# Causal attention on one NeuronCore: the diagonal blocks of a hybrid decoder layer without padding

## The chip, the cores and the metric

The kernel runs on one core of a Trainium2 chip. The metric is the device time of one execution in microseconds (us). Lower is better.

## The reference, cut to what matters

One decoder layer on 2048 tokens of 1024 features, in float32. Sixteen heads of 64 features: eight of forgetting attention (a softmax with a decay added to the logits) and eight of stick-breaking attention (sigmoids and a running product). Both are causal and take the queries in blocks of 128. Around them lie a projection, an output projection, and a gated MLP with a short convolution.

```python
def forgetting_attention(q, k, v, log_f):
    F = jnp.cumsum(log_f, axis=-1)
    ...
        s = jnp.einsum('bhqd,bhkd->bhqk', q_blk, k) * scale
        s = s + F_blk[..., None] - F[:, :, None, :]
        s = jnp.where(kpos[None, :] <= qpos[:, None], s, -jnp.inf)
        return jnp.einsum('bhqk,bhkd->bhqd', jax.nn.softmax(s, axis=-1), v)

def stick_breaking_attention(q, k, v):
    ...
        strict = kpos[None, :] < qpos[:, None]
        log_one_minus_beta = jnp.where(strict, jax.nn.log_sigmoid(-z), 0.0)
        rest = lax.cumsum(log_one_minus_beta, axis=3, reverse=True) - log_one_minus_beta
        a = jnp.where(strict, jnp.exp(jax.nn.log_sigmoid(z) + rest), 0.0)
        return jnp.einsum('bhqk,bhkd->bhqd', a, v)
```

For a query block t, key blocks beyond t are masked whole: they add nothing to the output.

## The kernel before, in words

The first 1520 us hold the projections and the attention, interleaved on TensorE; then come the output projection and the MLP, which the change does not touch.

**Number types.** Values are float32. Operands of most matmuls are kept in a rounded four-byte type (`fp32r`) as two parts, a rounded one and the rest, so that a product is made of two or three matmuls of that type. Transposes and a few small matmuls (the head variances at L716, the warm-up at L477) use plain float32. The trace names both types f32 on TensorE.

**Units and loops.** `attend` (L697) takes one unit: a kind, a pair of heads and 512 queries. It walks two pairs of query blocks (`j2`, with `j = 2 * tb + j2` from 0 to 7) and both heads of the pair. In all there are 8 pairs of heads, 4 values of `tb`, 2 of `j2` and 2 heads: 128 walks, 64 of them with an even j. One walk handles two query blocks (`qi` 0 and 1, key blocks up to 2j and up to 2j + 1) and accumulates into one PSUM bank `o`.

**Logits** (`logits`, L594): a chunk of up to 512 keys against 128 queries is two matmuls (L596, L597), the two parts of Q against K. The chunk needs `need` columns; in the last chunk `need` is (2j + qi + 1) * 128 less the keys of the chunks before. It is 128 for `qi` 0 where j is even. The matmuls are made `max(need, 2 * P)` wide (L627, L666), so at least 256 columns; the columns beyond `need` are not read. In the stick-breaking heads two sigmoids on ACT (L630, L631), a select on POOL (L633) and a scan on DVE (L636) follow; in the forgetting heads a fused add and minimum on DVE (L675) and an exponential on ACT (L679).

**Value matmuls** (`weighted`, L600): one step takes two key blocks (`kk` 0 and 1) and both query blocks. Four transposes on TensorE (L606) put the weights into a PSUM bank of four slots of 128 columns, in the order (kk 1, q 0), (kk 0, q 0), (kk 0, q 1), (kk 1, q 1). ACT copies them rounded into `at[:, 0]` (L610), DVE writes what is left into `at[:, 1]` (L611). Then four matmuls (L615), two key blocks times two parts, each with V as stationary operand and 256 columns of `at` streamed; for `kk` 1 the columns are the first and the last slot. `at` has three buffers, the PSUM tile `pt` three banks.

**The diagonal.** In the last step of a walk's keys (`kts[0] == 2 * j`) the block (kk 1, q 0) lies above the diagonal and is masked whole. Its transpose is left out, the eviction covers the other 384 columns, and ACT copies 128 zeros per part into its slot from a constant tile `edge` (L609), so that the matmuls of `kk` 1 keep their 256 columns.

**What orders the work.** Program order in `weighted` is as above. Projections of later units are fed in between by `interleave` and `pace` at set shares, some of them behind a logit matmul (`issue_after`, L1061). The order in which each engine finally takes its instructions is planned at build time by the tile framework from a modelled timeline (`schedule_with_timeline_sim=True`, L1758); engines then run in that order and wait on semaphores.

Of the kernel before, what the change touches and what calls it, by code (L numbers as in the profile page):

```python
# [12 lines left out]
AF = mybir.ActivationFunctionType  # L13
# [4 lines left out]
P = 128  # L18
# [16 lines left out]
def kernel(ctx: ExitStack, tc: tile.TileContext, x, c, w_ada, b_ada, g_attn, w_in, b_fgate,  # L35
                      g_out_fox, g_out_sb, w_out, g_mlp, w_up, conv_w, conv_b, w_down, g_final, out):
    nc = tc.nc
# [3 lines left out]
    def f(t):  # L41
        return t.bitcast(F32)
# [29 lines left out]
    edge = const.tile([P, TB + 1], F32, name="edge")  # L72
# [130 lines left out]
    last = {}  # L203
# [13 lines left out]
    b = pv()  # L217
# [6 lines left out]
    for r, src in ((R_GA, g_attn), (R_GM, g_mlp), (R_GF, g_out_fox), (R_GS, g_out_sb), (R_BA, b_ada)):  # L224
        n = src.shape[1] // P
# [368 lines left out]
    def logits(cw, qcols, hl, Q, K):  # L594
        b = qk()
        nc.tensor.matmul(b[:, :cw], Q[:, hl, 0, qcols], K[:, hl, :cw], start=True, stop=False)  # L596
        marks.append(nc.tensor.matmul(b[:, :cw], Q[:, hl, 1, qcols], K[:, hl, :cw], start=False, stop=True).ins)  # L597
        return b

    def weighted(o, kts, blk, V, hl, first, last, diag):  # L600
        b = pt()
        at = sb.tile([P, 2, 2 * 2 * P], F32R, name="at", tag="at", bufs=3)
        order = [(1, 0), (0, 0), (0, 1), (1, 1)]
        for i, (kk, qi) in enumerate(order):
            if not (diag and i == 0):
                nc.tensor.transpose(b[:, i * P:(i + 1) * P], blk(kts[kk], qi), ident)  # L606
        lo = P if diag else 0
        if diag:
            nc.scalar.activation(at[:, :, 0:P], edge[:, 0:2 * P].rearrange("p (a n) -> p a n", n=P), AF.Copy)  # L609
        copies = [nc.scalar.activation(at[:, 0, lo:], b[:, lo:], AF.Copy).ins,  # L610
                  nc.vector.tensor_sub(at[:, 1, lo:], b[:, lo:], f(at[:, 0, lo:])).ins]  # L611
        for kk, kt in enumerate(kts):
            for w in range(2):
                rhs = at[:, w].rearrange("p (s q) -> p s q", q=P)[:, 0:4:3, :] if kk else at[:, w, P:3 * P]
                m = nc.tensor.matmul(o[:, 0:2 * P], V[kt // 4][:, kt % 4, hl, :], rhs,  # L615
                                     start=first and kk == 0 and w == 0, stop=last and kk == 1 and w == 1)
        sums.append(m.ins)
        step[:] = [m.ins] + copies

    def sb_head(j, qc, hl, Q, K, V, o):  # L620
        n = (2 * j + 2 + 3) // 4
        right = [None, None]
        for ch in range(n - 1, -1, -1):
            at = []
            for qi in range(2):
                need = min(512, (2 * j + qi + 1) * P - ch * 512)
                b = logits(max(need, 2 * P), slice((qc + qi) * P, (qc + qi + 1) * P), hl, Q, K[ch])  # L627
                r = sx.tile([P, 512], F32, name="r", bufs=7)
                a = sx.tile([P, 512], F32, name="a", bufs=7)
                nc.scalar.activation(r[:, :need], b[:, :need], AF.Sigmoid)  # L630
                nc.scalar.activation(a[:, :need], b[:, :need], AF.Sigmoid, scale=-1.0)  # L631
                if right[qi] is None:
                    nc.gpsimd.affine_select(out=a[:, need - P:need], in_=a[:, need - P:need], pattern=[[-1, P]],  # L633
                                            base=-1, channel_multiplier=1, compare_op=ALU.is_ge, fill=0.0)
                rev = a[:, 0:need][:, ::-1]
                nc.vector.tensor_tensor_scan(rev, r[:, 0:need][:, ::-1], rev,  # L636
                                             0.0 if right[qi] is None else right[qi][:, 0:1], ALU.mult, ALU.add)
                right[qi] = a
                at.append(a)
            yield  # L640
            nk = min(4, 2 * j + 2 - 4 * ch)
            for m in range(0, nk, 2):
                kts = [4 * ch + m, 4 * ch + m + 1]
                weighted(o, kts, lambda kt, qi: at[qi][:, (kt - 4 * ch) * P:(kt - 4 * ch + 1) * P], V, hl,
                         ch == n - 1 and m == 0, ch == 0 and m == nk - 2, kts[0] == 2 * j)
                yield
# [10 lines left out]
    def fox_head(j, qc, hl, Q, K, V, o, Fb, ls):  # L657
        n = (2 * j + 2 + 3) // 4
        rows_ = []
        for qi in range(2):  # L660
            W = (2 * j + qi + 1) * P
            a = sx.tile([P, S], F32, name="p", bufs=4)
            mn = None
            for ch in range(n):
                need = min(512, W - ch * 512)
                b = logits(max(need, 2 * P), slice((qc + qi) * P, (qc + qi + 1) * P), hl, Q, K[ch])  # L666
                sl = slice(ch * 512, ch * 512 + need)
                m2 = sx.tile([P, 1], F32, name="mn", bufs=8)
                add = Fb[ch]
                if ch == n - 1:  # L670
                    add = px.tile([P, TB], F32, name="Fd", tag="hf_a", bufs=2)
                    mask[:] = [nc.gpsimd.affine_select(
                        out=add[:, :need], in_=Fb[ch][:, :need], pattern=[[-1, need]], base=need - P,
                        channel_multiplier=1, compare_op=ALU.is_ge, fill=BIG).ins]
                nc.vector.tensor_tensor_reduce(out=a[:, sl], in0=b[:, :need], in1=add[:, :need], scale=1.0,  # L675
                                               scalar=3e38 if mn is None else mn, op0=ALU.add, op1=ALU.min,
                                               accum_out=m2)
                mn = m2
            nc.scalar.activation(a[:, 0:W], a[:, 0:W], AF.Exp, scale=-1.0, bias=mn, accum_out=ls[:, hl, qc + qi:qc + qi + 1])  # L679
            rows_.append(a)  # L680
            yield
        for m in range(0, 2 * j + 2, 2):
            weighted(o, [m, m + 1], lambda kt, qi: rows_[qi][:, kt * P:(kt + 1) * P], V, hl, m == 0, m == 2 * j,
                     m == 2 * j)
            yield
# [11 lines left out]
    def attend(kind, p, tb, res, Fbs):  # L697
# [30 lines left out]
        for j2 in range(2):  # L728
            j = 2 * tb + j2
            for hl in range(2):  # L730
                o = pv()
                if kind == "sb":
                    yield from sb_head(j, 2 * j2, hl, Q, K, V, o)
                else:
                    yield from fox_head(j, 2 * j2, hl, Q, K, V, o, Fbs[hl], ls)
                o2 = sb.tile([HD, 2 * P], F32, name="o2", bufs=2)
                step[1] = nc.scalar.activation(o2, o[HD:P, 0:2 * P], AF.Copy).ins
                nc.vector.tensor_add(oT[hl * HD:(hl + 1) * HD, j2 * 2 * P:(j2 + 1) * 2 * P], o[0:HD, 0:2 * P], o2)
            head_var(j2)
# [86 lines left out]
    def attend_steps(u):  # L826
        kind, p, tb = u
        if kind == "fox":
            return sum(2 * (2 + 2 * tb + j2 + 1) for j2 in range(2)) + 1
        return sum(2 * (tb + 1 + 2 * tb + j2 + 1) for j2 in range(2)) + 1  # L830
# [199 lines left out]
    for i, u in enumerate(units):  # L1030
        kind, p, tb = u
# [10 lines left out]
        n = attend_steps(u)  # L1042
# [34 lines left out]
    def chunk(u, c):  # L1077
        t, n, q = ORDER.get(u, TURN)[c]
        if (t, n) not in banks:
            banks[t, n] = bank(psc, "bc", 2) if u == 1 and t == 0 else bank(psd, "o", 4)  # L1080
        with fixed():
            out_matmuls(u, banks[t, n], t, n, q)
        return t, n, q
# [171 lines left out]
    first = {"raw": [], "ws": []}  # L1255
# [41 lines left out]
    for u in range(1, NU):  # L1297
        for c in range(8 if u == 1 else 0, 16):
            t, n, q = chunk(u, c)
# [8 lines left out]
    def bank_a():  # L1308
        return bank(psd, "o", 4)
# [136 lines left out]
    for sblk, order in enumerate(orders):  # L1446
# [47 lines left out]
        a, b = bank_a(), bank_a()  # L1494
# [27 lines left out]
    def a_operand(i, s, kp, t):  # L1522
        nc.sync.dma_start(t, gs[kp][s][:, SUMS[i]])
        return operand(t)
# [17 lines left out]
    def raw_a():  # L1542
        return dp.tile([P, TB], F32, name="ra", bufs=5)
# [140 lines left out]
    for i in range(7):  # L1684
        nxt = {}
        kept = []
        for s in range(2):
# [4 lines left out]
            if left:  # L1692
                half, n = lefts[i]
                ops = left_over(s, half)
            for kp in range(NKP):
                a = ahead_a.pop((i, s, kp), None)
                if a is None:
                    a = a_operand(i, s, kp, raw_a())
                if kp not in bops:
                    bops[kp] = operand(b_block(i, kp, raw_b))  # L1700
                w = bops[kp]
# [60 lines left out]
```

## Time and profile before

| | |
|---|---|
| median of 3 runs | 2949.11 us (2948.72 to 2949.13) |
| the profiled execution | 2949.67 us |
| its span, first to last instruction | 2948.0 us |
| granted TensorE clock, mean | 0.99 of full speed |
| the stretch with the attention | 60 to 1520 us |
| ACT busy in that stretch | 1014.81 us |
| zero copies L609 | 128, first at 55.5 us, last at 1516.4 us |
| diagonal steps | 128 of 576 steps of `weighted` |

A row of a group reads: line, engine, operation, output and inputs by the program's names, shapes, count, then the busy time in us and the mean ns of one, then the idle time of the engine just before them with what ended it. A row of one line gives minimum, median and maximum duration in ns. "PE" is TensorE's matmuls, "PEld" its weight loads, which run beside matmuls. The duration of a matmul includes the way through the array, so the pace of a run of matmuls is shorter than their durations.

### The profile page before, as it was taken

How to read it: one execution, taken by the hardware profiler on the slowest of the kernel's cores; microseconds unless marked ns; L12 is line 12 of the kernel's file. 1: busy time of each engine (PE TensorE's matmuls, PEld its weight loads, DVE VectorE, ACT ScalarE, POOL GpSimd, SP SyncE). 2: the span in 40 equal slices, each digit the busy share in tenths (PEclk: the TensorE clock that was granted, in tenths of full speed). 3: DMA queues.
4: the chain of work that ended last, by engine and by line, in shares of the span. 5: the costliest groups of instructions: out<-in, count | busy, mean ns of one | idle time of the engine just before them, and what ended most of it. 6: DMA issues, size and time to landing. Idle time of an engine off the chain costs nothing.

```text
span 2948.0 us, 45934 instructions
## 1 busy us (share of the span) xinstructions
PE 2872.7 (97%) x15772; PEld 2466.9 (84%) x15772; DVE 2187.3 (74%) x3464; ACT 1689.3 (57%) x3187; POOL 899.8 (31%) x967
## 2 busy tenths in 40 slices
PE   8999999999999999999999999999999999999998
PEld 7888898888988889888788788888788888888887
DVE  5787778877877657658843688888998888575576
ACT  5776767777776666658743554444444444543342
POOL 0431312243022423231213344444254543142200
PEclk8999999999999999999999999999999999999999
DMA  9749756867469794794537765554744444975654
GB/s 292 254 133 328 221 196 210 298 202 234 151 217 355 252 296 145 231 323 140 182 115 232 250 219 134 136 136 125 230 134 128 129 133 129 301 266 189 212 159 148
DMA packets 348346, 601.89 MB, mean 204 GB/s; under 512 B 34672, under 2 KB 178800, under 8 KB 348112
## 3 DMA queue, kind: packets, MB, share of 16 engines
q1 hardware_dynamic: 324208, 558.06, 57.5%
q0 software_dynamic: 10880, 20.97, 4.4%
q10 hardware_dynamic: 13024, 19.93, 1.9%
q8 instruction: 124, 2.03, 0.3%
q14 instruction: 110, 0.90, 0.1%
HBM read 420.77 MB, written 177.02 MB: 203 GB/s over the span
## 4 chain that ended last, share of the span: by engine, by line
PE 48%; DVE 2%; DMA 2%; issue 1%; ACT 1%; SPq 0%; POOL 0%; DVEq 0%; ACTq 0%; POOLq 0%
PE ps_o L1316 19%; PE ps_t L1316 7%; PE ps_o L1613 6%; PE ps_t L1613 3%; PE ps_bc L1613 3%; PE ps_o L912 3%; PE ps_pv L615 2%; PE ps_pt L606 1%; PE ps_bc L912 1%; PE ps_qk L596 1%; DMA r<-rstd 1%; PE ps_o L1608 1%; DVE op L46 1%; PE ps_qk L597 1%; DMA hm<-hf_m 1%
## 5 line engine op out<-in xcount | busy, mean ns | idle before, releaser
L1316 PE MATMUL ps_o<-op,wu 128*128 128x512 f32 x2592 | 608.3, 389 | 2.0 <-DVE snap L1367 1.5
L1316 PEld LDWEIGHTS ps_o<-op,wu 128*128 128x128 f32 x2592 | 486.1, 188 | 103.9 <-DVE snap L1367 1.9
L611 DVE TENSOR_TENSOR at<-ps_pt,at 128x512 fp32r<-128x512 f32 (+1 forms) x576 | 365.8, 651 | 99.3 <-ACT at L610 96.8
L636 DVE TENSOR_TENSOR_SCAN a<-r,a 128x512 f32<-128x512 f32 (+2 forms) x320 | 368.7, 1168 | 76.6 <-ACT a L631 40.8
L342 PE MATMUL ps_pj<-hp,w_qk 128*128 128x512 f32 x1512 | 408.4, 401 | 11.0 <-DMA hp<-hs 8.6
L615 PE MATMUL ps_pv<-at,V 128*128 128x256 f32 x2304 | 405.5, 293 | 11.7 <-DVE at L611 4.7
L610 ACT ACTIVATE at<-ps_pt 128x512 fp32r<-128x512 f32 (+1 forms) x576 | 319.3, 576 | 139.2 <-PE ps_pt L606 123.0
L615 PEld LDWEIGHTS ps_pv<-at,V 128*128 128x128 f32 x2304 | 335.5, 191 | 44.9 <-DVE at L611 13.6
L342 PEld LDWEIGHTS ps_pj<-hp,w_qk 128*128 128x128 f32 x1512 | 274.7, 189 | 66.9 <-DMA hp<-hs 11.3
L596 PE MATMUL ps_qk<-K,Q 128*128 128x512 f32 (+2 forms) x640 | 266.8, 418 | 9.9 <-ACT a L631 4.7
L45 ACT ACTIVATE wu<-wuraw 128x512 fp32r<-128x512 f32 x204 | 128.8, 632 | 250.2 <-PE ps_o L1316 194.2
L413 PE MATMUL ps_pj<-w_v,hp 128*128 128x256 f32 (+1 forms) x1536 | 239.9, 290 | 1.3 <-DVE hp L422 0.9
L597 PE MATMUL ps_qk<-K,Q 128*128 128x512 f32 (+2 forms) x640 | 237.1, 372 | 0.0
L1316 PE MATMUL ps_t<-op,wu 128*128 128x512 f32 x888 | 220.5, 389 | 0.6 <-DVE op L46 0.6
L413 PEld LDWEIGHTS ps_pj<-w_v,hp 128*128 128x128 f32 x1536 | 211.7, 191 | 10.2 <-DVE q L373 1.3
L630 ACT ACTIVATE r<-ps_qk 128x512 f32<-128x512 f32 (+2 forms) x320 | 173.0, 541 | 59.7 <-PE ps_qk L597 57.0
L46 DVE TENSOR_TENSOR wu<-wuraw,wu 128x512 fp32r<-128x512 f32 x204 | 191.2, 937 | 18.2 <-ACT wu L45 17.0
L1316 PEld LDWEIGHTS ps_t<-op,wu 128*128 128x128 f32 x888 | 166.6, 188 | 35.6 <-DVE op L46 1.1
L606 PE MATMUL ps_pt<-edge,a 128*128 128x128 f32 x1088 | 186.0, 275 | 7.9 <-DVE a L636 7.4
L1613 PE MATMUL ps_o<-op 128*128 128x512 f32 x840 | 191.5, 389 | 0.0
L679 ACT ACTIVATE p<-p,mn 128x128 f32<-128x128 f32 (+15 forms) x128 | 153.9, 1203 | 56.4 <-DVE mn L675 54.8
L1613 PEld LDWEIGHTS ps_o<-op 128*128 128x128 f32 x840 | 157.7, 188 | 32.7
(338 smaller groups left out, 5215.5 us busy)
## 6 DMA issues: line engine op xcount, KB each, us to landing
hp<-hs SPq DMA_DIRECT2D x224, 512.0 KB
wuraw<-in_w_up_dram SPq DMA_DIRECT2D x80, 512.0 KB
ra<-g SPq DMA_DIRECT2D x136, 256.0 KB
rb<-in_w_down_dram SPq DMA_DIRECT2D x108, 256.0 KB
g<-u SPq DMA_DIRECT2D x80, 256.0 KB
hs<-hp SPq DMA_DIRECT2D x32, 512.0 KB
hp<-in_w_ada_dram SPq DMA_DIRECT2D x32, 512.0 KB
qk_fox<-q SPq DMA_DIRECT2D x32, 512.0 KB
```

The lines of the kernel that those rows point to most:

```text
L46: (lo_engine or nc.gpsimd).tensor_sub(lo, src, f(hi))
L342: nc.tensor.matmul(acc, w[kt][:, a, n], h[:, bb], start=kt == 0 and i == 0, stop=kt == KT - 1 and i == 2)
L413: nc.tensor.matmul(av[:, t * width:(t + 1) * width], hts[kt][:, a, tok], w[1][kt][:, bb, 0:width], start=kt == 0 and m == 0, stop=kt == KT ...
L596: nc.tensor.matmul(b[:, :cw], Q[:, hl, 0, qcols], K[:, hl, :cw], start=True, stop=False)
L597: marks.append(nc.tensor.matmul(b[:, :cw], Q[:, hl, 1, qcols], K[:, hl, :cw], start=False, stop=True).ins)
L606: nc.tensor.transpose(b[:, i * P:(i + 1) * P], blk(kts[kk], qi), ident)
L610: copies = [nc.scalar.activation(at[:, 0, lo:], b[:, lo:], AF.Copy).ins, nc.vector.tensor_sub(at[:, 1, lo:], b[:, lo:], f(at[:, 0, lo:])).ins]
L611: nc.vector.tensor_sub(at[:, 1, lo:], b[:, lo:], f(at[:, 0, lo:])).ins]
L615: m = nc.tensor.matmul(o[:, 0:2 * P], V[kt // 4][:, kt % 4, hl, :], rhs, start=first and kk == 0 and w == 0, stop=last and kk == 1 and w == 1)
L636: nc.vector.tensor_tensor_scan(rev, r[:, 0:need][:, ::-1], rev, 0.0 if right[qi] is None else right[qi][:, 0:1], ALU.mult, ALU.add)
L1316: nc.tensor.matmul(b, w[:, p, j], o[:, q], start=first and i == 0, stop=last and i == 2, skip_group_check=True)
L1613: nc.tensor.matmul(b, a[:, p, t * P:(t + 1) * P], w[:, q], start=first and i == 0, stop=last and i == 2, skip_group_check=True)
```

## The change

Three things, all in `weighted` and its callers. The zero copies are dropped. In a diagonal step the two matmuls of `kk` 1 take only the last slot (128 columns) and write only the second half of the output's 256 columns. The logit matmuls are `need` wide, so 128 columns where that is enough.

```diff
         lo = P if diag else 0
-        if diag:
-            nc.scalar.activation(at[:, :, 0:P], edge[:, 0:2 * P].rearrange("p (a n) -> p a n", n=P), AF.Copy)
         copies = [nc.scalar.activation(at[:, 0, lo:], b[:, lo:], AF.Copy).ins,
                   nc.vector.tensor_sub(at[:, 1, lo:], b[:, lo:], f(at[:, 0, lo:])).ins]
         for kk, kt in enumerate(kts):
             for w in range(2):
-                rhs = at[:, w].rearrange("p (s q) -> p s q", q=P)[:, 0:4:3, :] if kk else at[:, w, P:3 * P]
-                m = nc.tensor.matmul(o[:, 0:2 * P], V[kt // 4][:, kt % 4, hl, :], rhs,
-                                     start=first and kk == 0 and w == 0, stop=last and kk == 1 and w == 1)
+                c0 = P if diag and kk else 0
+                if diag and kk:
+                    rhs = at[:, w, 3 * P:]
+                else:
+                    rhs = at[:, w].rearrange("p (s q) -> p s q", q=P)[:, 0:4:3, :] if kk else at[:, w, P:3 * P]
+                m = nc.tensor.matmul(o[:, c0:2 * P], V[kt // 4][:, kt % 4, hl, :], rhs,
+                                     start=first and kk == 0 and w == 0, stop=last and kk == 1 and w == 1,
+                                     skip_group_check=True)
...
-                b = logits(max(need, 2 * P), slice((qc + qi) * P, (qc + qi + 1) * P), hl, Q, K[ch])
+                b = logits(need, slice((qc + qi) * P, (qc + qi + 1) * P), hl, Q, K[ch])
```

The last replacement is made twice, in `sb_head` (L627) and in `fox_head` (L666).

More of the change, by code (lines that the diff above doesn't have):

```diff
@@ L665, in fox_head @@
                 need = min(512, W - ch * 512)
-                b = logits(max(need, 2 * P), slice((qc + qi) * P, (qc + qi + 1) * P), hl, Q, K[ch])
+                b = logits(need, slice((qc + qi) * P, (qc + qi + 1) * P), hl, Q, K[ch])
                 sl = slice(ch * 512, ch * 512 + need)
```

## The prediction, made before the changed kernel ran

> **What bounds the kernel now.** I read the page's totals first, then the busy time by stretch, then the groups of instructions by shape, then the waits inside the attention stretch.
>
> ```profile
> span 2948.0 us, 45934 instructions
> PE 2872.7 (97%) x15772; PEld 2466.9 (84%) x15772; DVE 2187.3 (74%) x3464; ACT 1689.3 (57%) x3187; POOL 899.8 (31%) x967
> ...
> 60.00:1520.00 1460.00, 1412.06 (x9247) 1259.87 (x9247) 1084.86 (x1987) 1014.81 (x2084) 412.56 (x533) 0.99 0.67 224
> ```
>
> The first two lines are the page's totals; the third is the stretch from 60 to 1520 us, in which all the attention lies (its columns are PE, weight load, DVE, ACT and POOL busy time, granted clock, DMA share, GB/s). TensorE is busy for 1412.06 of 1460 us there, so at most 47.9 us of it are open idle time. DVE and ACT are at 74% and 70%: they matter only where TensorE waits for them. So the time is a sum of TensorE instructions, plus short stalls. These are the groups that the edit touches, by shape, for the matmuls and then for ACT:
>
> ```profile
> L615 PE MATMUL ps_pv<-at,V 128*128 128x256 f32 x2304 | 405.5, 293 | 11.7 <-DVE at L611 4.7 <-ACT at L610 3.5 <-DVE oT L738 2.6
> L596 PE MATMUL ps_qk<-K,Q 128*128 128x256 f32 x128 | 43.1, 339 | 6.5 <-DMA K<-q 2.4 <-ACT a L631 2.4 <-DVE mn L675 1.3
> L597 PE MATMUL ps_qk<-K,Q 128*128 128x256 f32 x128 | 36.8, 290 | 0.0
> ...
> L610 ACT ACTIVATE at<-ps_pt 128x384 fp32r<-128x384 f32 x128 | 62.5, 489 | 9.1 <-PE ps_pt L606 8.1
> L609 ACT ACTIVATE at<-edge 128x256 fp32r<-128x256 f32 x126 | 52.6, 417 | 18.8 <-PE ps_pv L615 17.9
> L630 ACT ACTIVATE r<-ps_qk 128x128 f32<-128x128 f32 x32 | 8.9, 279 | 9.8 <-PE ps_qk L597 9.4
> ```
>
> The 128 evictions of 384 columns (L610) count the diagonal steps: 128. The zero copies are L609 (126 of the 128 lie in this stretch). The 32 sigmoids of 128 columns (L630) count the stick-breaking blocks that need only 128 logits; the forgetting heads run the same loop over j, so there are 32 more, 64 in all.
>
> **The change, part by part: narrower matmuls.** Per diagonal step, the two value matmuls of the second key block go from 256 columns to 128: 2 x 128 = 256 of the 2304 at L615. Of the 256 logit matmuls of 256 columns (128 at L596, 128 at L597), the 64 blocks that need 128 go to 128 columns: 2 x 64 = 128. Together 384 matmuls lose half their width. No matmul of the rounded four-byte type (the fp32r tiles) with fewer than 256 columns is in this trace, so the price is bounded by its neighbours. What counts is the pace from start to start, which the timeline gives where instructions are merged (start, duration of the run of them, count):
>
> ```profile
> 705.18 1.11 PE L615 MATMUL ps_pv<-at,V 128*128 128x256 f32 x8
> ...
> 1018.67 0.82 PE L606 MATMUL ps_pt<-edge,p 128*128 128x128 f32 x6
> ...
> 1007.49 0.53 PEld L716 LDWEIGHTS ps_pt<-headsel,sq 128*128 128x128 f32 x4
> 1007.61 0.50 PE L716 MATMUL ps_pt<-headsel,sq 128*128 128x2 f32 x4
> ...
> 2520.31 27.20 PE ps_o L1613 x120
> ...
> L615 PEld LDWEIGHTS ps_pv<-at,V x2304: 186/188/337, 90.1 to 1518.7; 128*128 128x128 f32 x192
> L615 PE MATMUL ps_pv<-at,V x2304: 274/282/679, 90.2 to 1518.8; 128*128 128x256 f32 x192
> ...
> L606 PE MATMUL ps_pt<-edge,p x1088: 270/272/421, 879.1 to 1515.3; 128*128 128x128 f32 x182
> ...
> L716 PEld LDWEIGHTS ps_pt<-headsel,sq x252: 186/192/337, 128.8 to 1500.8; 128*128 128x128 f32 x126
> ```
>
> Eight value matmuls take 1.11 us, the last alone 0.28 us: (1.11 - 0.28) / 7 = 0.1186 us each. Six transposes of 128 columns: (0.82 - 0.27) / 5 = 0.110 us. The row that decides for me is L716: its matmuls stream 2 columns, almost nothing, yet their weight loads follow at (0.53 - 0.19) / 3 = 0.113 us. A weight load of 128 columns by itself paces TensorE at 0.113 us, its duration (median 192 ns) is that of L615's (188 ns), and every matmul here has a load of its own (15772 of each in the totals). So a 128-column value matmul waits for the next load instead of for its stream, and stops at 0.110 to 0.113 us. I take 0.1115, the middle: 0.1186 - 0.1115 = 0.007 us each, 384 x 0.007 = **2.7 us** saved. Ends of the unknown price: if a matmul's pace went with its width, 0.0593 us and 22.8 us saved; if a narrow one cost as much as a 512-column one (27.20 / 120 = 0.2267 us), 0.108 us more each, 41.5 us lost. The second end has a reason, in the rivals.
>
> The Trainium skill, page "TensorE: Matmul & The Clock Gate", section "Back-to-back issue gap", gives about 81 ns per matmul for a stream of load and matmul pairs of 128 columns; by that the saving would be 384 x 37.6 ns = 14.4 us. No row of this trace has pairs with a four-byte load at that pace: the 113 ns of L716 speaks against it.
>
> **The zero copies.** 128 ACT instructions of 417 ns go, 128 x 0.417 = 53.4 us of ACT. ACT is not the bound, so it is worth only what TensorE waits for ACT's queue. The waits of the weight load in the same stretch say how much that can be:
>
> ```profile
> PEld ps_pv L615 <- DVE at L611: 13.6, 34, 1.0
> ...
> PEld ps_pt L606 <- DVE a L636: 9.6, 14, 1.7
> PEld ps_qk L596 <- ACT a L631: 7.2, 10, 2.1
> ...
> PEld ps_pv L615 <- ACT at L610: 6.7, 11, 1.6
> ...
> PEld ps_pj L342 <- DMA hp<-hs: 11.3, 10, 3.8
> ```
>
> Columns are total us, times, longest. The copy stands ahead of the diagonal eviction on ACT; that eviction releases DVE's subtraction (L611), and both release the value matmuls: 13.6 + 6.7 = 20.3 us of waits over all 576 evictions. The diagonal ones are 128 / 576 = 22% of them: 20.3 x 0.22 = **4.5 us**, which I take as gained. The ends: nothing (ACT mostly waits for TensorE, and the copy fills an idle moment) and all four ACT and DVE waits, 13.6 + 9.6 + 7.2 + 6.7 = 37.1 us. L609 itself waited 17.9 us for value matmuls to release a buffer of `at`; that wait is not removed, it moves to the eviction, which needs the same buffer, though later. Behind the eviction on ACT stand the sigmoids and the exponentials, which no longer stand behind a copy that waits.
>
> **What else moves.** No DMA, DVE or POOL instruction is added or taken away, and no queue is passed. But each engine's order is planned when the program is built, from a modelled timeline that knows the widths and durations, so the whole stretch may come out in another order. I take that at nothing; the ends are plus and minus 11.3 us, the wait for the `hp` loads above, the largest wait of TensorE for something that only the order places. The strided operand becomes contiguous: the page shows no price for that, and the widest end is already in the price of the narrow matmuls. Everything after 1520 us is untouched.
>
> **The sum** stands against the profiled execution's own time, 2949.67 us (span 2948.0 and 1.7 around it), 0.56 us above the median of the runs, 2949.11. 2949.67 - 2.7 - 4.5 = 2942.5 us. Its own range: down by more of the 37.1 us and by a good order, up by no relief and a bad order: 2930 to 2956.
>
> **The rivals.** *A narrow matmul falls out of the fast rate (slower).* The rounded type streams one column where the plain four-byte type needs four times as long, and the trace has the plain one:
>
> ```profile
> L477 PE MATMUL ps_pj<-edge,ones x46: 379/379/794, 2.5 to 48.0; 128*128 128x256 f32 x46
> ...
> L1613 PE MATMUL ps_o<-op 128*128 128x512 f32 x840 | 191.5, 389 | 0.0
> ```
>
> A plain 256-column matmul (the warm-up, 23 calls in 46 records) is two records of 379 ns, each as long as a 512-column one of the rounded type (389 ns). So plain costs as much as four times the columns. If a rounded matmul below some width is run at the plain rate, 128 columns cost two 256-column streams, the pace of one of 512: 0.2267 us instead of 0.1186. The point from which it decides is anything under 256 columns at the four-fold rate: 384 x 0.108 = 41.5 us more TensorE time, in the stretch where TensorE is the bound and has 47.9 us idle scattered in pieces of a microsecond, which would hide little. With the 4.5 us of relief: 2949.67 + 41.5 - 4.5 = **2986.7 us**. For it: rounded matmuls of 256, 264, 384 and 512 columns all scale with width in the rows, and there is not one below. Against it: the fast rate is one record where the plain rate is two, so a narrow matmul would have to change its kind, and no row shows one that does.
>
> *The stream sets the pace (faster).* If the load could hide beside another matmul of the same queue and 128 columns took half of 0.1186: 22.8 + 4.5 us, **2922.4 us**. Against it: L716 above. By the Trainium skill's 81 ns (same page and section) it would be 2949.67 - 14.4 - 4.5 = 2930.8 us, an estimate from that page.
>
> *It does what it says, but nothing is waiting for it.* The 2.7 us remain and the relief is zero: 2947.0 us. For it: of ACT's idle time before the diagonal eviction, 8.1 of 9.1 us was ended by a transpose, so TensorE led there and ACT followed. This is the upper half of my own case.
>
> **How the numbers follow.** The load-bound case has a chance of 0.56 (faster by over 0.2% 0.33, within 0.17, slower 0.06 through the order alone); the four-fold rate 0.39, slower; the stream-bound case 0.05, faster. 0.2% is 5.9 us, about what a measurement of this kernel can tell from no change. That makes faster 0.38, same 0.17, slower 0.45. The predicted time is that of the likeliest case, 2942.5, though the other sign has much of the chance. The range must hold most of both cases: from 2932, which leaves out the stream-bound case and the best orders, to 2992, which takes in the four-fold rate with little relief (2949.67 + 41.5 = 2991.2).
>
> **What would show it.** The matmuls of 128 columns at L596, L597 and L615 appear as shapes of their own. Load-bound: their mean stays near L615's 293 ns or somewhat below, their loads follow at about 0.11 us. Four-fold: their durations rise to about 389 ns and pace to about 0.23 us. Stream-bound: runs of them at 0.06 to 0.08 us. Relief: ACT's 53 us go, and the weight load's waits at L615 fall from 20.3 by about 4.5 us; if the waits stay and appear under other releasers, the relief was hidden. I am wrong above all if a narrow matmul costs other than a load, or if the new order moves TensorE's idle time of 47.9 us by more than 10 us.

## The result, and the profile after

The changed kernel takes 2956.51 us (median of 20 runs, 2950.64 to 2967.0), against 2949.59 us for the kernel before (20 runs, 2943.74 to 2954.78). The ratio is 1.0024, interval 1.0016 to 1.0033: **slower by 7.1 us** (4.7 to 9.7). I had forecast 2942.5. One run of a later experiment, new order with old parts, took 3278.66 us at a granted clock of 0.812; its ratio leaves that run out.

The totals of the changed kernel's page, and its busy times from 60 to 1520 us (columns as before):

```profile
span 2960.2 us, 45789 instructions
PE 2879.7 (97%) x15772; PEld 2469.6 (83%) x15772; DVE 2178.6 (74%) x3464; ACT 1650.5 (56%) x3060; POOL 887.7 (30%) x967
```

```profile
60.00:1520.00 1460.00, 1407.85 (x9209) 1253.29 (x9208) 1076.43 (x1977) 973.23 (x1951) 396.44 (x528) 0.98 0.67 224
```

ACT lost 41.6 us of work in this stretch (1014.81 to 973.23), and TensorE stands open for 52.2 us of it instead of 47.9. Less work and more idle time. (This profiled execution took 2961.86 us, 5.4 above the median of the changed kernel's runs, at a granted clock of 0.986 against 0.990 in the one before.) The groups by shape show that the edit itself arrived as written:

```profile
L617 PE MATMUL ps_pv<-at,V 128*128 128x256 f32 x2048 | 378.7, 296 | 9.5 <-DVE at L609 5.3 <-DVE oT L741 2.0 <-ACT at L608 1.2
L617 PE MATMUL ps_pv<-at,V 128*128 128x128 f32 x256 | 43.1, 250 | 0.0
L597 PE MATMUL ps_qk<-K,Q 128*128 128x128 f32 x64 | 17.7, 277 | 0.0
L596 PE MATMUL ps_qk<-K,Q 128*128 128x128 f32 x64 | 17.4, 272 | 2.3 <-ACT a L634 1.7 <-DMA K<-q 0.4
```

In the changed kernel the value matmuls are L617, the eviction on ACT is L608, the subtraction on DVE L609. 256 + 64 + 64 = 384 matmuls are narrow, and their means (250 to 277 ns) lie below those of 256 columns (293 before). None is near 389, the length of a 512-column one. So a narrow matmul is not slow. What did grow are TensorE's waits. The weight load's waits from 60 to 1530 us (total us, times, longest):

```profile
PEld ps_pv L617 <- DVE at L609: 14.7, 33, 1.5
PEld ps_pj L342 <- DMA hp<-hs: 14.6, 13, 4.4
PEld ps_qk L596 <- ACT a L634: 10.8, 15, 2.6
PEld ps_qk L596 <- DVE mn L678: 8.8, 22, 1.1
...
PEld ps_pv L617 <- ACT at L608: 3.3, 9, 0.7
```

and the one row of before, from 60 to 1520 us, that the prediction did not need:

```profile
PEld ps_qk L596 <- DVE mn L675: 6.5, 15, 0.8
```

The value matmuls' wait fell by 2.3 us (13.6 + 6.7 to 14.7 + 3.3); the logits' waits rose by 5.9 (7.2 + 6.5 to 10.8 + 8.8) and the wait for `hp` loads by 3.3. Nothing in the edit makes the logits of the forgetting heads wait for DVE. The first suspect is the order, and it is only a suspect: these are rows of one execution each.

### The profile page after: what moved, and what is told of

The parts are those of the page before. It is cut to its first block, busy times and chain, and to the rows that moved or that the text cites. A ratio compares the mean times of both kernels' runs of the same rounds, so it can differ in the third digit from the quotient of the medians.

```text
span 2960.2 us, 45789 instructions
## 1 busy us (share of the span) xinstructions
PE 2879.7 (97%) x15772; PEld 2469.6 (83%) x15772; DVE 2178.6 (74%) x3464; ACT 1650.5 (56%) x3060; POOL 887.7 (30%) x967
## 4 chain that ended last, share of the span: by engine, by line
PE 81%; DMA 10%; DVE 4%; ACT 2%; issue 2%; SPq 1%; POOL 1%; DVEq 0%; ACTq 0%; POOLq 0%
PE ps_o L1319 19%; PE ps_pj L342 9%; PE ps_t L1319 7%; PE ps_pv L617 7%; PE ps_o L1616 6%; PE ps_pt L606 6%; PE ps_pj L413 5%; PE ps_qk L596 3%; PE ps_o L915 3%; PE ps_qk L597 3%; PE ps_t L1616 3%; PE ps_bc L1616 3%; DMA hp<-hs 2%; PE ps_bc L915 1%; DMA hp<-in_w_ada_dram 1%
## 5 line engine op out<-in xcount | busy, mean ns | idle before, releaser
L609 DVE TENSOR_TENSOR at<-ps_pt,at 128x512 fp32r<-128x512 f32 (+1 forms) x576 | 365.6, 651 | 109.3 <-ACT at L608 106.8
L342 PE MATMUL ps_pj<-hp,w_qk 128*128 128x512 f32 x1512 | 418.3, 407 | 13.5 <-DMA hp<-hs 10.6
L608 ACT ACTIVATE at<-ps_pt 128x512 fp32r<-128x512 f32 (+1 forms) x576 | 316.8, 576 | 184.5 <-PE ps_pt L606 155.9
L617 PE MATMUL ps_pv<-at,V 128*128 128x256 f32 (+1 forms) x2304 | 399.0, 291 | 9.5 <-DVE at L609 5.3
L617 PEld LDWEIGHTS ps_pv<-at,V 128*128 128x128 f32 x2304 | 337.3, 192 | 42.9 <-DVE at L609 14.7
L342 PEld LDWEIGHTS ps_pj<-hp,w_qk 128*128 128x128 f32 x1512 | 278.5, 192 | 71.1 <-DMA hp<-hs 14.6
L596 PE MATMUL ps_qk<-K,Q 128*128 128x512 f32 (+3 forms) x640 | 265.3, 415 | 11.7 <-ACT a L634 7.0
L597 PE MATMUL ps_qk<-K,Q 128*128 128x512 f32 (+3 forms) x640 | 236.4, 370 | 0.0
```

What stands on the lines that cost most here:

```text
L342: nc.tensor.matmul(acc, w[kt][:, a, n], h[:, bb], start=kt == 0 and i == 0, stop=kt == KT - 1 and i == 2)
L617: m = nc.tensor.matmul(o[:, c0:2 * P], V[kt // 4][:, kt % 4, hl, :], rhs, start=first and kk == 0 and w == 0, stop=last and kk == 1 and w ...
```

## The experiments

Two theories. **O**: the changed instructions are as cheap as forecast or cheaper, and the order that the planner made anew costs. **I**: the instructions themselves cost.

To tell them apart, I built each program twice: once to let the planner make its order for one set of parts (PLAN: zero copies, narrow value matmuls, narrow logits), then once more with the parts to be run (RUN), with every engine's instructions chained in the first order. A chain link only fixes the issue order, no engine waits through it. All instructions and their inputs are otherwise unchanged. Zero copies stand outside the chain: where RUN has them, the planner places them anew. The traces show that the order held: by operation and tile, TensorE's 15772 matmuls and DVE's 3464 instructions of old order with new parts come in the sequence of the kernel before, and those of new order with old parts in that of the changed kernel.

```diff
+                for k in order:
+                    x = plain[k]
+                    p = prev.get(x.engine)
+                    if p is not None:
+                        tc.add_manual_dep(x, p.name, _mybir.DependencyInfo(
+                            _mybir.DependencyClass.NoSync, _mybir.DependencyReason.DATA), reason="order")
+                    prev[x.engine] = x
...
+        PARTS = PLAN
+        order = build(None)[2]
+    PARTS = RUN
+    nc, arrays, done = build(order)
```

All ratios are against the kernel before on the same chip, five rounds each.

**Old order, new parts.**

```diff
+PLAN, RUN = (True, False, False), (False, True, True)
```

> The changed instructions (narrow value matmuls, narrow logits, no zero copies), but every engine takes them in the order that was planned for the kernel before. Theory O (the changed instructions are cheaper, and the re-planned order is what costs): faster than before by 2.7 to 7.2 us, ratio 0.9976 to 0.9991. Theory I (the instructions themselves cost, a narrow matmul being slow in some place or the chain of the diagonal tighter): slower than before by about 7 us, ratio about 1.0024, like the changed kernel.

Measured: 2950.0 us, ratio 1.0003 (0.9987 to 1.0019). The loss is gone; the gain that I forecast isn't there.

**New order, old parts.**

```diff
+PLAN, RUN = (False, True, True), (True, False, False)
```

> The instructions of before (256 columns everywhere, zero copies kept) in the order that was planned for the changed kernel; the 128 zero copies are placed by the planner. Theory O: slower than before by the loss of the changed kernel and the saving given back, 7 + 2.7 to 7.2 us, ratio 1.0033 to 1.0048. Theory I: about the time of before, ratio 1.000.

Measured: 2959.16 us, ratio 1.0030 (1.0016 to 1.0043). The old instructions in the new order lose as much as the changed kernel. Theory I falls. The weight load's waits from 60 to 1520 us (in us, one execution each) agree. The first two rows go with the order and not with the parts; the third, the wait for `hp` loads, goes with neither alone:

| TensorE's wait | before | old order, new parts | changed kernel | new order, old parts |
|---|---|---|---|---|
| value matmuls, for the eviction (ACT) and the subtraction (DVE) | 20.3 | 20.1 | 18.0 | 17.9 |
| logits, for ACT and DVE | 13.7 | 13.6 | 19.6 | 17.0 |
| projections, for `hp` loads | 11.3 | 14.0 | 14.6 | 14.8 |

The profiles also say where. The transposes of the forgetting heads (tile `p`) run from the first to the last of these times; the rows are those of the changed kernel, then of old order with new parts, then of new order with old parts:

```profile
L606 PE MATMUL ps_pt<-edge,p x1088: 270/272/474, 880.8 to 1524.9; 128*128 128x128 f32 x182
```

```profile
L611 PE MATMUL ps_pt<-edge,p x1088: 270/272/421, 876.5 to 1512.7; 128*128 128x128 f32 x182
```

```profile
L611 PE MATMUL ps_pt<-edge,p x1088: 270/272/417, 874.0 to 1518.0; 128*128 128x128 f32 x182
```

New order: 644.1 us and 644.0 us. Old order: 636.2 us, and 636.2 us in the kernel before (879.1 to 1515.3 in the prediction's row). In these four executions the 8 us go with the order, whatever the instructions are, and they arise in the forgetting heads. One place of it, in the timeline of the changed kernel:

```profile
907.07 1.40 DVE L752 SCALAR_TENSOR_TENSOR hp<-hp,cols 128x512 f32<-128x512 f32 x2
...
908.39 0.60 DVE L678 CUSTOM_DVE_ANT_0 p<-ps_qk,Fd,mn 128x384 f32<-128x384 f32 x1
...
909.06 0.19 PEld L596 LDWEIGHTS ps_qk<-K,Q 128*128 128x128 f32 x1 [1.07 <-DVE mn L678]
...
909.53 0.67 DVE L609 TENSOR_TENSOR at<-ps_pt,at 128x512 fp32r<-128x512 f32 x1
...
910.26 0.53 PEld L617 LDWEIGHTS ps_pv<-at,V 128*128 128x128 f32 x4 [0.90 <-DVE at L609]
```

and in that of new order with old parts, six microseconds earlier:

```profile
901.14 1.40 DVE L762 SCALAR_TENSOR_TENSOR hp<-hp,cols 128x512 f32<-128x512 f32 x2
...
902.46 0.60 DVE L688 CUSTOM_DVE_ANT_0 p<-ps_qk,Fd,mn 128x384 f32<-128x384 f32 x1
...
903.13 0.19 PEld L601 LDWEIGHTS ps_qk<-K,Q 128*128 128x128 f32 x1 [1.01 <-DVE mn L688]
...
904.33 0.54 PEld L627 LDWEIGHTS ps_pv<-at,V 128*128 128x128 f32 x4 [0.90 <-DVE at L617]
```

Two pieces of work for the output projection's weights, 1.40 us of DVE, are planned ahead of the reduction of the logits. That reduction frees the logits' PSUM bank late, and TensorE waits 1.0 to 1.1 us, then 0.9 us for the subtraction behind it. The same DVE instructions stand in the same order in both kernels, and the waits come at the same place with nearly the same lengths. In the old order no wait of that length is there. Over the whole stretch around this place (885 to 943 us) the same two waits come to this in the kernel before:

```profile
PEld ps_qk L596 <- DVE mn L675: 0.7, 2, 0.4
...
PEld ps_pv L615 <- DVE at L611: 0.3, 1, 0.3
```

Over the matching stretches they are 0.6 and 0.3 us in old order with new parts, 1.9 and 0.9 in the changed kernel, 1.7 and 0.9 in new order with old parts. So this place is about 2 of the 8 us; where the others arise was not traced.

**One part alone**, each with an order of its own.

```diff
+PLAN, RUN = None, (True, False, True)
```

> Only the first logits are made narrow (128 of the 384 matmuls); value matmuls and zero copies as before; order planned anew. Theory O: anything between 2 us faster and 10 us slower, since a new order is drawn; its stalls, not its matmuls, carry the difference. Theory I: a third of the changed kernel's loss or less, 0 to 2.4 us slower.

Measured: 1.0009 (0.9995 to 1.0022).

```diff
+PLAN, RUN = None, (False, True, False)
```

> Only the value matmuls are made narrow and the zero copies dropped; logits 256 columns as before; order planned anew. Theory O: anything between 6 us faster and 10 us slower, by the order drawn. Theory I: most of the changed kernel's loss, 4 to 7 us slower.

Measured: 0.9993 (0.9982 to 1.0004). Neither part has the loss, and their differences, 1.0009 and 0.9993, add up to 1.0002 and not to 1.0024: the parts don't add, as they would if they cost by themselves.

**The width by itself.** Order, logits and copies of before; all value matmuls but the first of each accumulation are narrow. This kernel leaves out the first half of the value output.

```diff
+                if NARROW_V == 2:
+                    c0 = 0 if first and kk == 0 and w == 0 else P
+                if NARROW_V == 2 and c0:
+                    rhs = at[:, w, 3 * P:] if kk else at[:, w, 2 * P:3 * P]
```

> Order of before, its logits and zero copies. 2176 of the 2304 value matmuls are made 128 columns wide (all but the first of each accumulation), so the first half of the value output is left out: it measures what width is worth on a chain of loads. Weight load sets the pace at 0.1115 us: 2176 x 0.007 = 15 us faster, ratio about 0.995. Pace goes with width: 2176 x 0.059 = 129 us faster, 0.956. Fourfold rate below 256 columns: 2176 x 0.108 = 235 us slower, 1.08.

Measured: 0.9967 (0.9955 to 0.9980), 9.7 us faster (5.9 to 13.3). A group of its profile, and two runs of narrow matmuls from its timeline:

```profile
L631 PE MATMUL ps_pv<-at,V 128*128 128x128 f32 x2176 | 334.1, 270 | 8.7 <-ACT at L616 4.1 <-DVE at L617 3.8
```

```profile
476.77 0.89 PE L631 MATMUL ps_pv<-at,V 128*128 128x128 f32 x7
...
488.01 1.00 PE L631 MATMUL ps_pv<-at,V 128*128 128x128 f32 x8
```

With 0.27 us for the last one, the mean pace is (0.89 - 0.27) / 6 = 0.103 and (1.00 - 0.27) / 7 = 0.104 us. The mean hides two values. Taken one by one from the trace, the starts follow each other after 57 and 60 ns once, behind the first narrow matmul, and after 109 to 115 ns from then on. So a run of narrow matmuls keeps the pace that I took (0.1115). That the load sets it is inferred: L716 keeps 0.113 with 2 columns.

In the change itself the narrow value matmuls come as pairs behind wide ones, not as runs. In old order with new parts the first of a pair is followed after 60 ns, the second after 113 (medians at full clock); before, the same two gaps are 119 and 120. That is 66 ns a pair where I had forecast 14. The next matmul takes some of it back (134 ns to its follower instead of 110), and over the nine gaps around a pair 33 ns remain (mean of the 81 pairs without a longer wait in either kernel): an estimate of 128 x 0.033 = 4.2 us. The weight load's waits of all kinds from 60 to 1520 us, 86.9 us before, are 91.5 in that kernel, so about as much came back as waiting.

In the whole kernel the all-narrow run keeps 9.7 / 2176 = 0.0045 us per matmul of the 0.007 forecast. By this rate the 384 matmuls of the change are worth 1.7 us. The rest of the 15 us may lie in the clock (below).

**The copies by themselves.** Order and matmuls of before, every zero copy made three times, then twice; the planner places the copies.

```diff
-            nc.scalar.activation(at[:, :, 0:P], edge[:, 0:2 * P].rearrange("p (a n) -> p a n", n=P), AF.Copy)
+            for _ in range(int(ZEROS)):
+                zc = nc.scalar.activation(at[:, :, 0:P], edge[:, 0:2 * P].rearrange("p (a n) -> p a n", n=P), AF.Copy)
```

> Order and matmuls of before, but every zero copy is made three times, so ACT has 256 more copies, 107 us. If the removed copies were worth the 4.5 us that I forecast, two more of each cost 9 us or more, ratio 1.003. If they stand in ACT's idle time, nothing: 0.999 to 1.001.

Measured: 1.0084 (1.0064 to 1.0104), 24.8 us slower.

> Order and matmuls of before, each zero copy made twice, 128 more copies, 53 us of ACT. With none of them the time was that of before, with three it was 24.8 us above. If the cost were linear from the second on: 12 us, ratio 1.004. If a second copy still fits into ACT's idle time: 0 to 4 us, 1.000 to 1.0014.

Measured: 1.0022 (1.0011 to 1.0032), 6.5 us slower. So the second copy costs 6.5 us and the third 18 more, while leaving out the first, together with the narrowing and in the same order, gave nothing that could be measured (1.0003). The diagonal eviction on ACT in old order with new parts, then the copies and the eviction when each copy is made three times, and the wait that grows there (0.4 us with two copies):

```profile
L616 ACT ACTIVATE at<-ps_pt 128x384 fp32r<-128x384 f32 x128 | 62.7, 491 | 28.8 <-PE ps_pt L611 21.9 <-PE ps_pv L627 2.4 <-DVE mn L688 2.3
```

```profile
L615 ACT ACTIVATE at<-edge 128x256 fp32r<-128x256 f32 x379 | 156.7, 420 | 22.0 <-PE ps_pv L628 18.4 <-issue 1.1
L617 ACT ACTIVATE at<-ps_pt 128x384 fp32r<-128x384 f32 x127 | 62.2, 490 | 3.3 <-PE ps_pt L611 2.3
```

```profile
PEld ps_pv L628 <- ACT at L615: 16.8, 12, 4.6
```

Before, ACT sat idle 18.8 us ahead of the copies and 9.1 us ahead of the diagonal evictions, 27.9 in all; without the copies it sits idle 28.8 us ahead of the evictions. So the 52.6 us of copies did not turn into idle time at this place: the evictions move up, and ACT is idle elsewhere. TensorE gains nothing by it because it takes the weights up later. In the trace of before, the first value matmul that needs DVE's subtraction in a diagonal step starts a median of 2.6 us after that subtraction has ended, and in only 11 of the 128 steps within 0.45 us, about the length of a copy. With three copies 3.3 us of idle time are left ahead of the evictions, and value matmuls wait 16.8 us for copies themselves. Where the 6.5 us of the second copy go these waits do not show.

**Which engines' order.** New parts; TensorE alone held to the old order, then all but TensorE.

```diff
                     x = plain[k]
+                    if str(x.engine) != "EngineType.PE":
+                        continue
```

> The changed instructions; TensorE alone is held to the order planned for the kernel before, and ACT, DVE, POOL and the DMA queues are planned anew around it. If the loss lies in the order of the matmuls: about the time of before, 0.999 to 1.001. If it lies in the order of the evictions, scans and loads: slower, 1.002 to 1.003.

Measured: 1.0054 (1.0039 to 1.0069).

```diff
                     x = plain[k]
+                    if str(x.engine) == "EngineType.PE":
+                        continue
```

> The reverse: ACT, DVE, POOL and the DMA queues held to the order planned for the kernel before, TensorE planned anew. If the loss lies in the order of the matmuls: 1.002 to 1.003. If in that of the others: 0.999 to 1.001. Both about 1.000 would say that the two orders have to drift together.

Measured: 1.0002 (0.9992 to 1.0013). With the old order of ACT, DVE, POOL and the DMA queues and a new one for TensorE the loss is gone; with the old order of matmuls alone it is larger than ever, 15.9 us. So the loss goes with the order in which the engines around TensorE serve it, as far as two runs can tell: each of them is again one draw for the part that is planned anew.

**Is the new order worse for a reason?** The rest are orders planned for other parts and run with the changed kernel's instructions. First three that were planned with narrow values, with all narrow but copies kept, and with nothing narrow:

```diff
+PLAN, RUN = (False, True, False), (False, True, True)
```

> All the changed instructions (narrow logits too), in the order that was planned for the kernel with narrow value matmuls and no zero copies but logits of 256 columns. Theory O: the order carries the time, so this is within 2 us of that kernel's 2948.2, minus about 1 us for 128 narrower logit matmuls; ratio to before 0.998 to 1.000, and about 9 us faster than the changed kernel, with which it shares every instruction. Theory I: about the changed kernel's ratio, 1.0024.

Measured: 0.9997 (0.9986 to 1.0007).

```diff
+PLAN, RUN = (True, True, True), (False, True, True)
```

> All the changed instructions, in the order that was planned for the kernel with all matmuls narrow but the zero copies kept. Theory O, as a draw of an order: between 0.998 and 1.004. A variant of O, that narrow widths in the planner's model of time make its orders worse: about 1.0024 or more. A variant that the missing copies do: about 1.000. Theory I: 1.0024.

Measured: 1.0039 (1.0024 to 1.0053).

```diff
+PLAN, RUN = (False, False, False), (False, True, True)
```

> All the changed instructions, in the order planned for the kernel without zero copies but with 256 columns everywhere. Theory O, as one more draw: 0.998 to 1.004. If it is the narrow widths in the planner's model of time that make its orders worse: about 1.000, since no width is narrow in this plan. If the missing copies do: about 1.0024.

Measured: 1.0001 (0.9990 to 1.0013). Both orders planned with 128 columns everywhere were slow, the others not. So I varied the width that the planner was told for the 384 matmuls, and ran them at 128. The diff is that of width 160; the other five only have another number.

```diff
-PLAN, RUN = (False, False, False), (False, True, True)
+PLAN, RUN = (False, 160, 160), (False, 128, 128)
...
+                    c0 = max(0, c1 - NARROW_V)
+                    c1 = c0 + NARROW_V
+                    rhs = at[:, w, 4 * P - NARROW_V:]
...
```

> Every instruction is that of the changed kernel; only the order differs: it is the one planned for a kernel whose narrow matmuls are 160 columns wide. If the planner's orders are worse because of narrow widths in its model of time: 1.002 to 1.004, like the two orders planned with 128 columns everywhere (1.0024, 1.0039). If an order is a draw: anywhere from 0.999 to 1.004, without a trend in the width.

> As the run of width 160, order planned for 192 columns. By widths: about half of the loss, 1.001 to 1.002. By draw: 0.999 to 1.004.

> As the run of width 160, order planned for 224 columns. By widths: little loss, 1.000 to 1.001. By draw: 0.999 to 1.004.

> As the run of width 160, order planned for 264 columns, wider than before. By widths: no loss, 0.999 to 1.000. By draw: 0.999 to 1.004.

> All instructions of the changed kernel, order planned as if its narrow matmuls were 320 columns wide. From 128 to 264 columns of planned width the ratios ran from 1.0024 and 1.0039 over 1.0009, 1.0016, 1.0007 and 1.0001 to 0.9982. If this is a trend (the planner leaves more room behind a matmul that it takes for slower): 0.997 to 0.999. If the orders are draws: 0.998 to 1.004, most likely above 0.999.

> As the run of width 320, planned with 384 columns. Trend: 0.996 to 0.999. Draws: 0.998 to 1.004, most likely above 0.999.

| order planned for a width of | ratio to before | interval |
|---|---|---|
| 128 (the changed kernel) | 1.0024 | 1.0016 to 1.0033 |
| 160 | 1.0009 | 0.9999 to 1.0019 |
| 192 | 1.0016 | 1.0003 to 1.0029 |
| 224 | 1.0007 | 0.9995 to 1.0020 |
| 264 | 0.9982 | 0.9971 to 0.9993 |
| 320 | 0.9998 | 0.9988 to 1.0007 |
| 384 | 1.0033 | 1.0022 to 1.0044 |

Up to 264 columns it looked like a trend, and I expected it to go on. It didn't: 384 is as slow as 128. The nearest account is a draw: 13 orders of the same instructions (these seven, and those of the runs above that have all the new parts) lie between 0.9982 and 1.0054, their mean at 1.0013. Whether widths near the true ones make better orders on average isn't settled by seven. Two of the 13 hold only a part of the engines to an order.

The forgetting heads do not explain all 13. From the first to the last of their transposes, the four slowest (1.0024 and above) take 641.2 to 644.1 us and six of those near 1 (0.9997 to 1.0009) take 632.9 to 636.9. But the orders planned for 192, 224 and 264 columns take 639.6 to 644.3 us, and the last of them is the fastest of all: other stretches make up for it.

The order planned for 264 columns is the version that beats both kernels: 2945.85 us (11 runs), 5.3 us faster than before (2.1 to 8.6). It is the best of 13 and so partly luck.

**The granted clock.** One thing is held fixed by no run. Each lists its mean granted TensorE clock, and this moves with the kernel: it is 0.9909 to 0.9913 on average for the kernel before, on four chips, and 0.9889 for the changed kernel. Among the runs of one and the same kernel, 0.001 less of it goes with 2.1 us more (334 runs, each set against its own kernel's mean). By this estimate 4 to 5 of the 7.1 us go with the lower clock. In the traces it is a matter of stretches at half clock, each 3.4 us long or a multiple of that: 20.5 us of them in the forgetting heads of the changed kernel, 10.3 before, 10.7 in old order with new parts, 8.9 in new order with old parts. So the changed kernel's 644.1 us and the 644.0 of the old parts are not made of the same pieces, and their agreement is partly chance.

The order costs at an equal clock too, by the same estimate: new order with old parts (0.9897, on average 8.9 us above before) would be 5.6 us slower, old order with new parts (0.9901, 2.1 us above) 0.4 us faster. The all-narrow run has the lowest clock, 0.9871; at that of before its narrow matmuls would be worth some 18 us, near the 15 forecast. Why these kernels are granted less is not shown, nor whether the lower clock is a part of what an order costs or only comes with it.

## Why the prediction was wrong

- **The narrow matmul** (2.7 us saved, load-bound): the pace of a run of them came out as taken, 0.109 to 0.115 us. In the pairs of the change the first gap is 0.060 us, the 0.0593 of the stream-bound rival, and only the second is load-bound; the following matmul gives part of it back. The worth in the whole kernel was 0.0045 us per matmul, 1.7 us for the change. The fourfold rival (41.5 us lost, chance 0.39) and the stream-bound one (22.8 us) both fell by the all-narrow run, which would have been 235 us slower or 129 us faster. The 81 ns of the Trainium skill ("TensorE: Matmul & The Clock Gate", "Back-to-back issue gap") does not hold for a run of these four-byte operands: the trace shows 109 to 115, and the measurement decides.
- **The zero copies** (4.5 us of relief): the size was wrong. I took 22% of all evictions' waits, as if each of those waits had a copy ahead of it. At a held order the waits of the value matmuls stayed (20.3 to 20.1 us), and the whole change came out at 1.0003, which leaves room for 3.8 us gained at most, for widths and relief together. In 117 of 128 diagonal steps TensorE came for the subtraction's result more than 0.45 us after it was ready. The row that I quoted against myself, 8.1 of 9.1 us of idle time before the diagonal eviction ended by a transpose, pointed the right way.
- **The step that failed**: "I take that at nothing", of the order that is planned anew, "the ends are plus and minus 11.3 us". The 13 orders lay between 5.3 us below and 15.9 us above the time of before, so the bound was nearly right (two lie beyond its upper end, at 11.5 and 15.9). Taking nothing as the value was what failed: this order cost 6.2 us with the new parts (1.0003 to 1.0024) and 8.9 with the old (1.0030). Of the 14.3 us between the forecast change (7.2 faster) and the measured one (7.1 slower), 6.2 are the order, and the other 8.1 are the saving, which at a held order did not come (0.9 us slower, 3.8 faster to 5.6 slower). It took both to turn the sign. I gave "slower" a chance of 0.06 inside the load-bound case, against 0.33 for "faster by over 0.2%". Of the 13 orders, all with the new parts, four were slower by over 0.2% and none was faster by that much.
- The granted clock stood in no term of the sum. It was lower in the changed kernel, and how much of the order's cost it carries stays open.
- The range (2932 to 2992) held the time by luck: its upper end stood for the fourfold rate, and the load-bound case's own range (2930 to 2956) ends just below the 2956.51 measured. That "slower" had the largest chance (0.45) was luck as well, as 0.39 of it stood for that rate.

## What to carry to other kernels

Where a planner writes each engine's order, an edit that touches a few per cent of the instructions draws a new order for all of them, and here such draws differ by 0.7% with every instruction the same (ratios to before, each good to about 0.1%). So an edit worth less than that is judged at a held order first (here the changed parts in the old order: no difference), and orders are then tried for themselves. An instruction taken from an engine off the bound is worth nothing until the trace shows who waits behind it: look at how long its result lies ready before it is taken up (here a median of 2.6 us). And compare the granted clock of two kernels before you explain the last microseconds between them.

## What the runs showed of the hardware that I had not expected

- In a run of matmuls of the rounded four-byte type with 128 columns, each with a load of its own, starts follow each other after 0.109 to 0.115 us, against 0.1186 for 256 columns. Half the columns are worth about 6% of the pace there. Only the first one behind a wider one is followed after 0.057 to 0.060 us, about half of 0.1186. No run shows this type at a slower rate below 256 columns.
- ACT work costs nothing and then a lot: leaving out 128 copies of 417 ns (with the narrowing) changed nothing at the same order, 128 more cost 6.5 us, and the 128 after them 18 us, at the same matmuls.
- Programs with the same instructions and different issue order differ by up to 21 us of 2949 (0.9982 to 1.0054) on one core.
- The mean granted clock differs between kernels that differ only in widths or order: from 0.9871 (all value matmuls narrow) to 0.9921 (order planned for 320 columns), where 0.001 goes with about 2.1 us.
